# A decoder layer on one core: half of the first modulation slice's product on TensorE, and slices of 3, 5, 4 and 4 row tiles

## The chip, the cores and the metric

The kernel runs on one core of one Trainium2 chip. The metric is the device time of one launch in microseconds, as the median of several runs. Engines are named as the profile names them: PE is the matrix engine (PEld its weight loads), DVE the vector engine, ACT the scalar engine, POOL the general-purpose one, SP the engine whose queue issues most transfers.

## The reference, cut to what matters

One layer on 256 tokens of 2048 columns, all in float32. `mod` comes from one conditioning vector `c`; its first two of six parts shift and scale the first norm, whose result `h` meets the wide input matrix.

```python
mod = jax.nn.silu(c) @ w_ada[layer] + b_ada[layer]
sh1, sc1, g1, sh2, sc2, g2 = [m[:, None, :] for m in jnp.split(mod, N_MOD, axis=-1)]
h = rms_norm(x, norm1_gain[layer]) * (1.0 + sc1) + sh1
x = x + g1 * hybrid_mixer(h, positions, w_in[layer], ...)
...
proj = h @ w_in
```

`w_ada` is 2048 x 12288. The mixer (gated linear attention, sparse attention, a gated merge), the second norm, the feed-forward part and the last norm follow; the change leaves them alone.

## The kernel before

**Products.** Weights are streamed once, in chunks of at most four row tiles (128 rows) by 512 columns. Each float32 chunk is split: ACT casts it to a float32r part `hi` (L303), DVE subtracts to get the exact rest `lo` (L305), in halves of at most 1024 columns. For every row tile and each of two token tiles PE makes three products (L345 to L347): `h_hi*hi`, `h_hi*lo`, `h_lo*hi`, 512 columns each. Four halves of `hi` and of `lo` exist, and chunks are split two ahead of their products.

**The first stage.** The first 6144 columns of `w_in` are multiplied in slices over the 16 row tiles of `h` (`INIT_KTS`, 4 + 4 + 4 + 4 before), so that products can begin when a quarter of the modulation is known. A slice is 12 groups of 512 columns. The first slice leaves its results in SBUF by ACT; the later ones are added by DVE (L529). After the four slices comes the `Lr` chunk (L327, L328), and then the rest of the layer.

**The modulation of a slice.** `w_ada` is read as `(p j)`: partition p holds 16 rows j, and `sc[:, j]` is the silu of `c` for them. A piece (`Ada`) is some j of the shift and scale columns of the slice. DVE multiplies by `sc` (L283 for j = 0) and adds up (L285, a scalar_tensor_tensor) in `acc`, one instruction for each j. What remains is a sum over the partitions: `column_sums` transposes each 128 x 128 block on PE (L481) and DVE reduces it (L482); `mod_columns` then makes A and B (L455 to L457), and `modulated` makes the two parts of `h` (ACT L464, DVE L468 and L471 in the first slice).

**Order.** Nothing is scheduled behind the program's back: each engine executes in the order in which the code issues. The first slice's eight pieces come first, each issued as two transfers; the pieces of slice s + 1 are spread over the first eight groups of slice s (`ADA_DONE`, some groups earlier by `ADA_LEAD`), and DVE's work on them stands between the halves of `lo`. All raw chunks and pieces pass through six buffers in this stage, in the order of use; SP's queue loads one when its last reader is done. `first_norm` (ACT squares, POOL, ACT scales `xs`) and `transpose_x` (32 PE transposes, L491, and eight ACT copies, L495) stand ahead of the first pieces in the code, so PE does them as soon as ACT has scaled `xs`.

Of the kernel before, what the change touches and what calls it, by code (L numbers as in the profile page):

```python
# [23 lines left out]
RAW_BUFS = 3          # raw chunks of weights in flight  # L24
EARLY_RAWS = 3        # and more of them while the working tiles of later stages are not there yet
HL_BUFS = 4           # halves of split chunks
AHEAD = 2             # chunks split ahead of their products
INIT_KTS = (4, 4, 4, 4)    # row tiles of the slices of the first products
ADA_DONE = 8          # the group of a slice before which the next slice's modulation is loaded and then applied
ADA_LEAD = (0, 2, 4)  # groups by which each slice's pieces of it start early  # L30
MID = 2               # row tile of the last chunk before which the first token tile's norm goes on
# The second norm's steps (512 columns, token tile) after the first two, with p for a half of a split,
# and the steps done before each row tile of the chunks that read them.
NORM_STEPS = "p 01 11 p p 20 21 30 31"
NORM_DONE = "0000 1233 3333 4557 7777 7777"
SLOT = 3.6            # vector engine time for the threads beside a chunk, in us
# [9 lines left out]
class Mm:  # L46
    """A chunk of a weight matrix: nk row tiles of 128, nc columns, for a group of products.

    With defer, the second token tile waits until a later chunk with by_token has done the first one.
    With home, its parts are in the tiles that home makes and not in the ring of all chunks.  # L50
    """
# [19 lines left out]
class Ada:  # L71
    """A piece of w_ada: nj of every partition's 16 rows, nc columns from c0 on of nseg segments."""

    def __init__(self, c0, nc, nseg, j0, nj, acc, pre=None):
        self.c0, self.nc, self.nseg, self.j0, self.nj, self.acc, self.pre = c0, nc, nseg, j0, nj, acc, pre
        self.by_seg = False

# [6 lines left out]
class Thread:  # L84
# [6 lines left out]
    def step(self):  # L91
        """The next step's cost, which it yields, or None at the end."""
        while True:
            if self.cur is None:
                if not self.q:
                    return None
                self.cur = self.q.popleft()
            try:
                return next(self.cur) or 0.0
            except StopIteration:  # L100
                self.cur = None
# [7 lines left out]
def tile_layer(tc, x, c, positions, norm1_gain, norm2_gain, w_ada, b_ada, w_in, gate_up, gate_bias,  # L109
# [3 lines left out]
    with (  # L113
# [42 lines left out]
        # ------------------------------------------------------------ constants and small inputs  # L156
# [36 lines left out]
        # rotary tables  # L193
# [22 lines left out]
        def rstd_of(ss, n, k):  # L216
            """(ss / n + eps) ^ -0.5 in place, k columns."""
            pool.tensor_scalar(ss, ss, 1.0 / n, EPS, ALU.mult, ALU.add)
            pool.tensor_tensor(ss, ss, half[:, 0:k], ALU.pow)

        def mean_of_three(ss):
            """ss[:, :, 0] becomes the part of mean + eps of the first three of four sums, for last_rstd."""
            pool.tensor_tensor(ss[:, :, 0], ss[:, :, 0], ss[:, :, 1], ALU.add)
            pool.tensor_tensor(ss[:, :, 0], ss[:, :, 0], ss[:, :, 2], ALU.add)
            pool.tensor_scalar(ss[:, :, 0], ss[:, :, 0], 1.0 / D, EPS, ALU.mult, ALU.add)
# [5 lines left out]
        # ------------------------------------------------------------ the stream of weights  # L231
# [42 lines left out]
        def pre_ada(it):  # L274
            if it.pre:
                it.pre()
            a = it.acc()
            segs = [slice(i, i + 1) for i in range(it.nseg)] if it.by_seg else [slice(0, it.nseg)]
            for g in segs:
                for j in range(it.nj):  # L280
                    s = sc[:, it.j0 + j:it.j0 + j + 1]
                    if it.j0 + j == 0:
                        dve.tensor_scalar_mul(a[:, g], it.raw[:, j, g], s)  # L283
                    else:
                        dve.scalar_tensor_tensor(a[:, g], it.raw[:, j, g], s, a[:, g], ALU.mult, ALU.add)  # L285
                    yield

        def pre_mm(it, rests_last=False):
            """The float32 chunk into its float32r part and the exact rest, a step for each half."""
            it.hl = []  # L290
            nk, ncol = (KT, 128) if isinstance(it, Lr) else (it.nk, it.nc)
            per = min(nk, 1024 // ncol)
            home = [h().rearrange("p (k n) -> p k n", k=nk) for h in getattr(it, "home", ())]
            rests = []
            for k in range(0, nk, per):
                src = it.raw[:, k:k + min(per, nk - k)]
                m = src.shape[1]
                if home:
                    hv, lv = (h[:, k:k + m] for h in home)
                else:  # L300
                    hv, lv = (stp.tile([128, 1024], F32R, tag=v, bufs=HL_BUFS, name=name(v))[:, 0:m * ncol]
                              .rearrange("p (k n) -> p k n", k=m) for v in ("hi", "lo"))
                act.copy(hv, src)  # L303
                it.hl.append((hv, lv))
                rests.append(lambda lv=lv, src=src, hv=hv: dve.tensor_sub(lv, src, hv.bitcast(F32)))  # L305
                if not rests_last:
                    rests.pop()()
                    yield
            for rest in rests:
                yield  # L310
                rest()

        def pre(its):
            """The pieces of its, a step of each in turn: steps of one piece of w_ada depend on each other."""
# [47 lines left out]
        def run():  # L362
# [36 lines left out]
            def pre_steps(**order):  # L399
                """The next chunk's pieces, a step at a time."""  # L400
# [38 lines left out]
        # ------------------------------------------------------------ first norm and its modulation  # L439
# [13 lines left out]
        def mod_columns(ps, n, A, B, bsc, bsh, gain):  # L453
            """A = (1 + scale) * gain and B = shift of n row tiles, from ps = [shift | scale]."""
# [4 lines left out]
        def modulated(kts, h, A, B, temp, on_act, between=None):  # L459
            """The transposed tokens in xs into the parts of h at the row tiles kts."""  # L460
# [14 lines left out]
        def column_sums(blocks, dst):  # L475
            """The sums of blocks [128, 128] over the partitions, a column of dst for each."""
# [7 lines left out]
        def transpose_x():  # L484
            """xs in place into its transposes, tiles [128, 256] for the row tiles; no block is overwritten before it is read."""
            pts = {}
            for k in range(0, KT, 2):
# [5 lines left out]
                for w in sorted(pts):  # L493
                    if min(2 * w + 4, KT) <= k + 2:
                        act.copy(xs[w // 8][:, (w % 8) * S:(w % 8 + 2) * S], pts.pop(w))  # L495

        def init_columns(s, k0, nk):
            a2 = init_acc(s, nk)
            pc = cp.tile([128, 2 * nk], F32, name=name("pc"))
            column_sums([a2[:, seg, a * 128:(a + 1) * 128] for seg in range(2) for a in range(nk)], pc)  # L500
# [48 lines left out]
        def first_transposes():  # L549
            first_norm()  # L550
            transpose_x()

        items.append(Call(first_transposes))
        items.extend(init_ada(*slices[0]))
        items[-1].by_seg = True
# [32 lines left out]
        # ------------------------------------------------------------ gated linear attention  # L588
# [179 lines left out]
        # ------------------------------------------------------------ indexer  # L768
        def rope(v, nh, dh, rot, step):
            """Rotates the first rot of dh in each of nh heads, in place, on both token tiles."""  # L770
# [100 lines left out]
        # ------------------------------------------------------------ sparse attention  # L871
# [3 lines left out]
        def seg_start(i):  # L875
            """Before the first piece of a segment: what the last one left is reduced."""
# [20 lines left out]
        def reduce_rows(dst, n):  # L897
            """A slice of 512 of the sums over the partitions added to dst, on every partition."""
# [112 lines left out]
        # ------------------------------------------------------------ branches, gates and merge  # L1011
# [32 lines left out]
        def split_transposes(src, kt0, dst):  # L1044
            """Transposes [128, 2, 512] into row tiles kt0.. of the parts in dst, in two steps."""
# [94 lines left out]
        # ------------------------------------------------------------ second norm  # L1140
        def second_norm(last):
# [17 lines left out]
            def modulate(n, t, ps, a0, na):  # L1159
                """Row tiles of one token tile; the second token tile's products are on the other engine."""  # L1160
# [61 lines left out]
        # ------------------------------------------------------------ feed-forward  # L1222
# [55 lines left out]
        def final_token(t):  # L1278
            """The last norm of a token tile; the columns before the last 512 have their gain already."""
# [54 lines left out]
def constants():  # L1334
    """Constants of the shapes alone: the identity, the masks of the decay's levels, the rotary frequencies."""
# [37 lines left out]
```

## Time and profile before

| | us |
|---|---|
| median of 3 runs | 1889.79 (1889.21 to 1892.36) |
| profiled execution, first to last instruction | 1885.6 |
| median less that span | 4.2 |
| PE busy in the span | 1834.9 (97%) |
| DVE busy | 1286.0 (68%) |
| ACT busy | 854.0 (45%) |

The profiled execution has no time of its own beside its span; 4.2 us is what lies around the span if it ran as the median does. Busy shares are over the whole span, while the change touches its first sixth.

### The profile page before, as it was taken

How to read it: one execution, taken by the hardware profiler on the slowest of the kernel's cores; microseconds unless marked ns; L12 is line 12 of the kernel's file. 1: busy time of each engine (PE TensorE's matmuls, PEld its weight loads, DVE VectorE, ACT ScalarE, POOL GpSimd, SP SyncE). 2: the span in 40 equal slices, each digit the busy share in tenths (PEclk: the TensorE clock that was granted, in tenths of full speed). 3: DMA queues.
4: the chain of work that ended last, by engine and by line, in shares of the span. 5: the costliest groups of instructions: out<-in, count | busy, mean ns of one | idle time of the engine just before them, and what ended most of it. 6: DMA issues, size and time to landing. Idle time of an engine off the chain costs nothing.

```text
span 1885.6 us, 23215 instructions
## 1 busy us (share of the span) xinstructions
PE 1834.9 (97%) x9148; PEld 1510.9 (80%) x9148; DVE 1286.0 (68%) x1442; ACT 854.0 (45%) x1115; POOL 138.3 (7%) x201
## 2 busy tenths in 40 slices
PE   3999999999999999999999999999999999999998
PEld 3888888777788888888888787888788888888886
DVE  6899865788866678777777656677555444554455
ACT  4554444655645444344344446444333444334443
POOL 0000000543220110200000000000000000000002
PEclk8999999999999999999999999999999999999999
DMA  9998843543444787878888754888555555555553
GB/s 369 387 345 315 282 161 104 182 154 135 150 164 156 270 298 280 300 269 300 305 312 312 275 193 164 318 328 314 178 200 191 189 189 191 186 194 194 185 180 133
DMA packets 198046, 440.84 MB, mean 234 GB/s; under 512 B 7816, under 2 KB 14112, under 8 KB 188848
## 3 DMA queue, kind: packets, MB, share of 16 engines
q1 hardware_dynamic: 196544, 433.69, 65.5%
q10 hardware_dynamic: 1392, 5.66, 0.8%
q8 instruction: 72, 1.18, 0.2%
q14 instruction: 38, 0.31, 0.0%
HBM read 437.22 MB, written 2.10 MB: 233 GB/s over the span
## 4 chain that ended last, share of the span: by engine, by line
PE 78%; issue 12%; DVE 3%; POOL 3%; ACT 2%; DMA 1%; SPq 0%; POOLq 0%; ACTq 0%; DVEq 0%
PE pm L345 25%; PE pm L347 25%; PE pm L346 25%; DVE acc L285 1%; PE pa L1050 1%; DVE lo L305 1%; ACT hi L303 1%; POOL tm L782 1%; POOL rp L783 1%; POOL rp L780 0%; POOL rp L781 0%; PE ph L679 0%; POOL rp L779 0%; DMA raw<-in_w_ada_dram 0%; PE pa L901 0%
## 5 line engine op out<-in xcount | busy, mean ns | idle before, releaser
L305 DVE TENSOR_TENSOR lo<-raw,hi 128x1024 fp32r<-128x1024 f32 (+1 forms) x632 | 768.0, 1225 | 537.1 <-ACT hi L303 536.7
L303 ACT CAST hi<-raw 128x1024 fp32r<-128x1024 f32 (+1 forms) x632 | 652.6, 1041 | 898.8 <-PE pm L347 714.6
L345 PE MATMUL pm<-hi,h 128*128 128x512 f32 (+1 forms) x1784 | 699.0, 392 | 2.2 <-ACT h L464 1.9
L347 PE MATMUL pm<-hi,h 128*128 128x512 f32 (+1 forms) x1784 | 690.5, 387 | 0.0
L346 PE MATMUL pm<-lo,h 128*128 128x512 f32 (+1 forms) x1784 | 689.6, 387 | 0.2 <-DVE lo L305 0.2
L345 PEld LDWEIGHTS pm<-hi,h 128*128 128x128 f32 x1784 | 335.9, 188 | 70.1 <-ACT h L464 2.3
L347 PEld LDWEIGHTS pm<-hi,h 128*128 128x128 f32 x1784 | 335.5, 188 | 68.9 <-DVE h L471 0.2
L346 PEld LDWEIGHTS pm<-lo,h 128*128 128x128 f32 x1784 | 336.0, 188 | 66.1 <-DVE lo L305 0.9
L345 PE MATMUL pm<-hi,gA 128*128 128x512 f32 x608 | 242.1, 398 | 0.0
L347 PE MATMUL pm<-hi,gB 128*128 128x512 f32 x608 | 237.0, 390 | 0.0
L346 PE MATMUL pm<-lo,gA 128*128 128x512 f32 x608 | 236.8, 389 | 0.1
L285 DVE SCALAR_TENSOR_TENSOR acc<-raw,sc,acc 128x2048 f32<-128x2048 f32 (+2 forms) x122 | 218.2, 1789 | 3.5 <-DMA raw<-in_w_ada_dram 2.6
L346 PEld LDWEIGHTS pm<-lo,gA 128*128 128x128 f32 x608 | 114.2, 188 | 25.1 <-issue 1.7
L345 PEld LDWEIGHTS pm<-hi,gA 128*128 128x128 f32 x608 | 114.2, 188 | 24.7 <-issue 1.9
L347 PEld LDWEIGHTS pm<-hi,gB 128*128 128x128 f32 x608 | 114.1, 188 | 24.2
L1274 POOL TENSOR_TENSOR gC<-gC,gr 128x512 f32<-128x512 f32 x3 | 4.9, 1640 | 716.9 <-ACT pm L1272 716.9
L663 POOL TENSOR_TENSOR acc<-gC 128x512 f32<-128x512 f32 x32 | 40.0, 1260 | 34.0 <-DVE acc L672 33.6
L672 DVE TENSOR_TENSOR acc<-gB,acc 128x256 f32<-128x256 f32 x64 | 32.3, 565 | 6.9 <-ACT acc L667 6.8
L779 POOL TENSOR_TENSOR rp<-tm,cos 128x64 f32<-128x64 f32 x18 | 12.2, 677 | 297.8 <-ACT tm L927 180.1
L981 ACT ACTIVATE S<-S,mx 128x128 f32<-128x128 f32 (+1 forms) x32 | 14.3, 448 | 32.8 <-DVE mx L979 32.8
L667 ACT ACTIVATE acc<-acc 128x256 f32<-128x256 f32 x64 | 22.3, 416 | 9.7 <-POOL acc L663 9.6
L345 PE MATMUL pm<-hi,gr 128*128 128x512 f32 x64 | 24.9, 389 | 0.0
(271 smaller groups left out, 1066.6 us busy)
## 6 DMA issues: line engine op xcount, KB each, us to landing
raw<-in_w_in_dram SPq DMA_DIRECT2D x129, 1024.0 KB, 4.9
raw<-in_w_ffn_gate_up_dram SPq DMA_DIRECT2D x88, 1024.0 KB, 4.9
raw<-in_w_ada_dram SPq DMA_DIRECT2D x64, 1024.0 KB, 4.8
raw<-in_w_ffn_down_dram SPq DMA_DIRECT2D x44, 1024.0 KB, 5.2
raw<-in_w_ada_dram SPq DMA_DIRECT2D x64, 512.0 KB, 8.5
raw<-in_w_branch_gla_dram SPq DMA_DIRECT2D x16, 1024.0 KB, 5.3
raw<-in_w_branch_dsa_dram SPq DMA_DIRECT2D x16, 1024.0 KB, 5.3
raw<-in_w_merge_out_dram SPq DMA_DIRECT2D x16, 1024.0 KB, 5.4
```

Source lines behind the costliest of these rows:

```text
L285: dve.scalar_tensor_tensor(a[:, g], it.raw[:, j, g], s, a[:, g], ALU.mult, ALU.add)
L303: act.copy(hv, src)
L305: rests.append(lambda lv=lv, src=src, hv=hv: dve.tensor_sub(lv, src, hv.bitcast(F32)))
L345: pe.matmul(o, a, hv, start=it.first and k == 0, stop=False)
L346: pe.matmul(o, a, lv, start=False, stop=False)
L347: pe.matmul(o, b, hv, start=False, stop=it.last and k == it.nk - 1)
L663: pool.tensor_tensor(d, v, v[:, :, s - 1:s].to_broadcast([128, n, 2 * s]), ALU.subtract)
L667: act.activation(d, d, AF.Exp, scale=(1.0 if u else -1.0) / 16)
L672: dve.tensor_tensor(w, src, d, ALU.mult)
L782: pool.tensor_tensor(a, u[0], u[1], ALU.subtract)
L783: pool.tensor_tensor(u[0], b, co, ALU.mult)
L1050: pe.transpose(ps[:, a * S + t * 128:a * S + t * 128 + 128], src[:, t, (i * 2 + a) * 128:(i * 2 + a + 1) * 128], ident)
```

## The change

`INIT_KTS` becomes `(3, 5, 4, 4)`. For the first slice, the rows j = 1 of each of the eight pieces (two j each, 768 columns now) go to PE instead of DVE: for each of the six blocks of 128 columns a float32 product with the 128 x 128 block of raw weights as the stationary operand and `sc[:, j]`, one column, as the moving one, added up in one PSUM tile `pc`. DVE adds up the rows j = 0 alone. Then six products with a column of ones add DVE's sums over the partitions to `pc`, in place of transposes and reductions, and `mod_columns` reads PSUM. The x transposes are issued in eight steps, two behind each of the second to the fifth piece. The last piece is no longer taken segment by segment.

The second slice has five row tiles: its modulation comes in 16 pieces of one j and 1280 columns, and its groups in chunks of four and of one row tile.

```diff
-INIT_KTS = (4, 4, 4, 4)    # row tiles of the slices of the first products
+INIT_KTS = (3,5,4,4)
...
                     s = sc[:, it.j0 + j:it.j0 + j + 1]
+                    if j in it.on_pe:
+                        for i in range(2):
+                            for k in range(it.nc // 128):
+                                c = i * it.nc // 128 + k
+                                pe.matmul(state["pc"][:, c:c + 1], it.raw[:, j, i, k * 128:(k + 1) * 128], s,
+                                          start=c == 0 and it.j0 + j == it.on_pe[0], stop=False)
+                        continue
...
         def init_columns(s, k0, nk):
             a2 = init_acc(s, nk)
-            pc = cp.tile([128, 2 * nk], F32, name=name("pc"))
-            column_sums([a2[:, seg, a * 128:(a + 1) * 128] for seg in range(2) for a in range(nk)], pc)
+            blocks = [a2[:, seg, a * 128:(a + 1) * 128] for seg in range(2) for a in range(nk)]
+            if s == 0:
+                pc = state["pc"]
+                for i, b in enumerate(blocks):
+                    pe.matmul(pc[:, i:i + 1], b, ones[:, 0:1], start=False, stop=i == 2 * nk - 1)
+            else:
+                pc = cp.tile([128, 2 * nk], F32, name=name("pc"))
+                column_sums(blocks, pc)
...
-        items.append(Call(first_transposes))
-        items.extend(init_ada(*slices[0]))
-        items[-1].by_seg = True
+        items.append(Call(first_steps))
+        for i, it in enumerate(init_ada(*slices[0])):
+            it.on_pe = (1,)
+            items.append(it)
+            if 1 <= i <= 4:
+                items.append(Call(lambda: [next(state["x_steps"]) for _ in range(2)]))
         items.append(Call(first_slice))
```

PE at the start of the program, before: the last x transposes (L491), the transposes of DVE's sums (L481), and the first products.

```order
L491 MATMUL pm_198<-cc,gB_76 128x128
L491 MATMUL pm_198<-cc,gB_77 128x128
L491 MATMUL pm_198<-cc,gB_76 128x128
L491 MATMUL pm_198<-cc,gB_77 128x128
L481 MATMUL pa_254<-cc,acc 128x128 x4
L481 MATMUL pa_260<-cc,acc 128x128 x4
L345 MATMUL pm_319<-hi_247,h_105 128x512
L346 MATMUL pm_319<-lo_248,h_105 128x512
L347 MATMUL pm_319<-hi_247,h_105 128x512
```

PE in the change, the same place (the lines are numbered anew: L287 is a product with `sc`, L500 an x transpose, L513 a product with ones, L353 the first product): from the last x transposes to the first products.

```order
L500 MATMUL pm_248<-cc,gB_76 128x128
L500 MATMUL pm_248<-cc,gB_77 128x128
L500 MATMUL pm_248<-cc,gB_76 128x128
L500 MATMUL pm_248<-cc,gB_77 128x128
L287 MATMUL ph_136<-sc,raw_133 128x1 x6
L287 MATMUL ph_136<-sc,raw_168 128x1 x6
L287 MATMUL ph_136<-sc,raw_178 128x1 x6
L513 MATMUL ph_136<-ones,acc 128x1 x6
L353 MATMUL pm_354<-hi_287,h_105 128x512
L354 MATMUL pm_354<-lo_288,h_105 128x512
L355 MATMUL pm_354<-hi_287,h_105 128x512
```

Behind the last x transpose PE now has 24 small float32 products to issue before the first main product, where before it had eight transposes. At the front of its queue it has twelve, ahead of the first x transpose:

```order
L287 MATMUL ph_136<-sc,raw_118 128x1 x6
L287 MATMUL ph_136<-sc,raw_121 128x1 x6
L500 MATMUL pa_181<-cc,gB_76 128x128
L500 MATMUL pa_181<-cc,gB_77 128x128
L500 MATMUL pa_181<-cc,gB_76 128x128
L500 MATMUL pa_181<-cc,gB_77 128x128
```

The products on the first two pieces stand in front; those on pieces three to five stand between the x transposes, six behind every eight.

DVE, before, behind the first slice's `h`: the work on slice 1's pieces and the splits of groups 1 and 2 of slice 0 (L283 and L285 on pieces, L305 makes `lo`).

```order
L283 TENSOR_SCALAR acc<-raw_224,sc 128x1024
L305 TENSOR_TENSOR lo_291<-raw_229,hi_290 128x1024
L285 SCALAR_TENSOR_TENSOR acc<-raw_224,sc,acc 128x1024
L305 TENSOR_TENSOR lo_296<-raw_229,hi_295 128x1024
L285 SCALAR_TENSOR_TENSOR acc<-raw_233,sc,acc 128x1024
L305 TENSOR_TENSOR lo_306<-raw_238,hi_305 128x1024
L285 SCALAR_TENSOR_TENSOR acc<-raw_233,sc,acc 128x1024
L305 TENSOR_TENSOR lo_311<-raw_238,hi_310 128x1024
```

DVE in the change, the same place (L291, L293 on pieces, L313 makes `lo`):

```order
L291 TENSOR_SCALAR acc<-raw_219,sc 128x1280
L293 SCALAR_TENSOR_TENSOR acc<-raw_240,sc,acc 128x1280
L313 TENSOR_TENSOR lo_321<-raw_265,hi_320 128x1024
L313 TENSOR_TENSOR lo_325<-raw_265,hi_324 128x512
L293 SCALAR_TENSOR_TENSOR acc<-raw_274,sc,acc 128x1280
L293 SCALAR_TENSOR_TENSOR acc<-raw_284,sc,acc 128x1280
L313 TENSOR_TENSOR lo_339<-raw_315,hi_338 128x1024
L313 TENSOR_TENSOR lo_343<-raw_315,hi_342 128x512
L293 SCALAR_TENSOR_TENSOR acc<-raw_328,sc,acc 128x1280
L293 SCALAR_TENSOR_TENSOR acc<-raw_331,sc,acc 128x1280
```

Two pieces of 1280 columns, one instruction each, now stand ahead of a group's two `lo` halves (1024 and 512 columns), where one piece of two instructions of 1024 columns stood beside two halves of 1024.

## Rows read from the trace of the kernel before

**Rows 1.** The page: its head, and busy time, share and instructions by engine.

```profile
span 1885.6 us, 23215 instructions
PE 1834.9 (97%) x9148; PEld 1510.9 (80%) x9148; DVE 1286.0 (68%) x1442; ACT 854.0 (45%) x1115; POOL 138.3 (7%) x201
```

**Rows 2.** Timeline of PE (start, length): first of slice 1; end of the stage.

```profile
106.94 0.39 PE L345 MATMUL pm<-hi,h 128*128 128x512 f32 x1
...
305.31 0.39 PE L347 MATMUL pm<-hi,h 128*128 128x512 f32 x1
305.54 0.39 PE L327 MATMUL pm<-h,hi 128*128 128x512 f32 x1
```

**Rows 3.** Timeline of all engines, the first 45 us; bracketed: idle before, and releaser.

```profile
12.16 0.75 DVE L283 TENSOR_SCALAR acc<-raw,sc 128x1024 f32<-128x1024 f32 x1 [4.16 <-DMA raw<-in_w_ada_dram]
...
15.27 19.16 DVE L285 SCALAR_TENSOR_TENSOR acc<-raw,sc,acc 128x1024 f32<-128x1024 f32 x16 [1.03 <-DMA raw<-in_w_ada_dram]
...
19.05 0.90 PE L491 MATMUL pa<-cc,gB 128*128 128x128 f32 x3 [1.42 <-ACT gB L451]
...
19.75 1.06 PE L491 MATMUL pm<-cc,gB 128*128 128x128 f32 x4
...
23.56 0.60 PE L491 MATMUL pa<-cc,gB 128*128 128x128 f32 x4
...
34.10 1.99 ACT L303 CAST hi<-raw 128x1024 fp32r<-128x1024 f32 x2 [7.04 <-DMA raw<-in_w_in_dram]
...
35.69 0.69 DVE L482 TENSOR_REDUCE pc<-pa 128x4 f32<-128x512 f32 x1 [0.67 <-PE pa L481]
...
37.52 0.80 PE L345 MATMUL pm<-hi,h 128*128 128x512 f32 x1 [1.87 <-ACT h L464]
...
39.08 0.33 PEld L345 LDWEIGHTS pm<-hi,h 128*128 128x128 f32 x1
...
42.19 0.75 DVE L283 TENSOR_SCALAR acc<-raw,sc 128x1024 f32<-128x1024 f32 x1
```

**Rows 4.** Stretches of 10 us, columns as in the first row.

```profile
core 0: us, PE busy (x) PEld busy (x) DVE busy (x) ACT busy (x) POOL busy (x), PEclk, DMA share, GB/s
0.00:10.00 10.00, 0.69 (x2) 0.36 (x2) 0.32 (x1) 4.71 (x13) 0.43 (x6) 1.00 0.82 307
10.00:20.00 10.00, 1.42 (x6) 1.13 (x7) 6.62 (x6) 5.80 (x9) 2.97 (x5) 1.00 1.04 384
20.00:30.00 10.00, 4.59 (x28) 4.35 (x26) 9.47 (x8) 4.30 (x8) 0.00 (x0) 0.99 1.05 387
30.00:40.00 10.00, 4.48 (x13) 2.99 (x14) 8.94 (x18) 4.53 (x7) 0.00 (x0) 0.50 1.05 387
40.00:50.00 10.00, 10.00 (x38) 8.10 (x37) 9.90 (x12) 4.60 (x6) 0.00 (x0) 0.82 1.05 387
```

**Rows 5.** Weight loads by line and shape: count, busy us, mean ns of one.

```profile
L345 PEld LDWEIGHTS pm<-hi,h 128*128 128x128 f32 x1784 | 335.9, 188 | 70.1 <-ACT h L464 2.3 <-issue 2.1 <-ACT hi L303 1.1
...
L693 PEld LDWEIGHTS pa<-acc 128*128 128x128 f32 x16 | 2.4, 190 | 0.3
...
L698 PEld LDWEIGHTS pa<-acc 128*64 128x64 f32 x32 | 2.2, 137 | 0.5
```

**Rows 6.** Timeline of PE around 372 us: two kinds of float32 product.

```profile
372.36 0.60 PE L693 MATMUL pa<-acc 128*128 128x128 f32 x4
372.89 0.68 PE L698 MATMUL pa<-acc 128*64 128x64 f32 x8
```

**Rows 7.** DVE by line and shape, 37 to 310 us: the split at two widths.

```profile
L305 DVE TENSOR_TENSOR lo<-raw,hi 128x876 fp32r<-128x876 f32 x1 | 1.1, 1074 | 0.2 <-ACT hi L303 0.2
...
L305 DVE TENSOR_TENSOR lo<-raw,hi 128x292 fp32r<-128x292 f32 x1 | 0.5, 464 | 1.1 <-ACT hi L303 1.1
```

**Rows 8.** Chain that ended last, 145 to 165 us: start, length, engine, tile.

```profile
155.37 1.14 DVE lo L305
156.50 1.20 DVE acc L285
```

More of the change, by code (lines that the diff above doesn't have):

```diff
@@ L76, in __init__ @@
         self.by_seg = False
+        self.on_pe = ()
 class Call:
@@ L486, in transpose_x @@
             pts = {}
+            yield
             for k in range(0, KT, 2):
@@ L495, in transpose_x @@
                         act.copy(xs[w // 8][:, (w % 8) * S:(w % 8 + 2) * S], pts.pop(w))
+                yield
         def init_columns(s, k0, nk):
             a2 = init_acc(s, nk)
-            pc = cp.tile([128, 2 * nk], F32, name=name("pc"))
-            column_sums([a2[:, seg, a * 128:(a + 1) * 128] for seg in range(2) for a in range(nk)], pc)
+            blocks = [a2[:, seg, a * 128:(a + 1) * 128] for seg in range(2) for a in range(nk)]
[6 more added lines that the diff above has]
+                column_sums(blocks, pc)
             kk = slice(k0, k0 + nk)
@@ L548, in tile_layer, with first_steps @@
             k0 += nk
-        def first_transposes():
+        def first_steps():
+            state["pc"] = psum_held()
             first_norm()
-            transpose_x()
-        items.append(Call(first_transposes))
-        items.extend(init_ada(*slices[0]))
-        items[-1].by_seg = True
+            state["x_steps"] = transpose_x()
+            next(state["x_steps"])
+        items.append(Call(first_steps))
[4 more added lines that the diff above has]
+                items.append(Call(lambda: [next(state["x_steps"]) for _ in range(2)]))
         items.append(Call(first_slice))
```

## The prediction

> **What bounds the kernel now.** I read the page first: PE is busy for 97% of a span of 1885.6 us [rows 1], so a gain must come from when PE starts, or from waits of PE. Then the timeline of the start and of the stage's end: the first product starts at 37.52 us [rows 3], slice 1 at 106.94, and the stage's last product ends where `Lr` begins, at 305.54 [rows 2]. The reader is to see that from 37.52 on PE hardly waits: the 864 products of slices 1 to 3 (36 groups of 24) take 198.6 us, 0.230 us each with all gaps. Everything behind 305.54 is work of PE that the change leaves alone, so I let the shift of that point pass through to the end one to one. The question is thus one number: when does the last product of the first stage end?
>
> Before 37.52 the chain is: pieces of `w_ada`, DVE's 16 instructions on them (15.27 to 34.4), transposes and reductions to 36.38, A and B, `h`. Beside it the first weight chunk lands only at 34.10 (ACT's cast waited 7.04 us for it) [rows 3]. The transfers run at 384 to 387 GB/s from 10 us on, whatever the engines do [rows 4]: the queue is full. That is the second limit.
>
> **The yardstick.** After the change slices 1 to 3 have 13 row tiles, 936 products: 936 x 0.230 = 215.2 us. So the stage ends as before if slice 0 ends (the end of its 216 products) at 305.5 - 215.2 = 90.3 us.
>
> **Part 1: when the first product starts.** The pieces hold 0.79 MB instead of 1.05 MB, so the first lands some 0.7 us earlier than the 12.16 of now, at 11.5 us, and one more each 2.03 us at 387 GB/s, the eighth at 25.7. DVE has one instruction for each piece and is done about 27. That would save much; but PE now has 54 products with one moving column, none of which the trace shows.
>
> Their price. A float32 product is recorded as two passes, each with its own load of the stationary block (L693: eight products in the code, 16 loads [rows 5]). One moving column costs next to nothing, so the load of 128 columns sets the pace. The mean load takes 190 ns for 128 columns and 137 for 64 [rows 5]: 0.83 ns a column, so 106 ns for 128 beside a fixed part that overlaps. Upper bound: L693, which loads 128 and streams 128 columns, steps (0.60 - 0.27)/3 = 0.11 us a pass (0.27 is the length of one, and the last of the four hardly overlaps) [rows 6]; with fewer streamed columns a pass can't be dearer. Lower bound: if the load went at the pace at which a main product streams 512 columns in 0.23 us, 0.45 ns a column, a pass would take 0.058 us. L698, with half the columns on both sides, steps (0.68 - 0.22)/7 = 0.066 [rows 6], which fits the dear end. I take 0.107 a pass, 0.21 us a product at the full clock, 0.43 at the lower level: the load of a main product is recorded with 0.33 us at 39.08 [rows 3] and 0.188 in the mean [rows 5], and four transposes take 1.06 us at 19.75 and 0.60 at 23.56 [rows 3], 0.213 and 0.11 each.
>
> The sum on PE. The first two pieces' 12 products are done at 16.7 even at the lower level (2.56 us each from 11.5). The x transposes wait for ACT until 19.05 as now [rows 3]; nothing moves there. From 19.05 PE has 32 transposes and 42 products in a row: 3.5 + 8.8 = 12.3 us at the full clock, plus some 0.9 if the clock rises only during the first of them (before, the step fell at about 23): 32.3. No data is late for it. From the end of the sums to the first product it now takes 37.52 - 36.38 = 1.1 us: **first product at 33.4**, 4.1 us earlier. What is late next is PE itself; at a lower price it would be the first weight chunk: 9.5 MB in all, landed at 28, cast by 29.6, first product at 30.
>
> By the way the clock stands: PE ran only transposes between 19 and 25 us, and the step fell to 0.11 while they ran, with the granted clock at 0.99 for 20 to 30 us, and 0.50 for 30 to 40, after a pause [rows 3, 4]; the main products before 43 us ran at the lower level. The Trainium skill (TensorE: Matmul & The Clock Gate, PE-mode transpose) says that the full clock does not engage for transposes. By that rule the 32 transposes would stay at 0.213 us, and the first product would come at 35.8 instead of 33.4; this trace disagrees, and I go by it.
>
> **Part 2: slice 0 itself.** A group is now 18 products, 4.14 us of PE. For each of the first eight groups DVE has two pieces of 1280 columns and two halves of `lo`. In the chain `lo` of 1024 columns takes 1.14 us and an addition of 1024 takes 1.20 [rows 8]; a column costs (1074 - 464)/584 = 1.04 ns [rows 7]. So: 2 x 1.47 + 1.14 + 0.61 = 4.69, plus about 0.1 because the two additions to one `acc` now stand side by side (16 in 19.16 us at the start, four of them half as long [rows 3], are slower than 1.20 each): 4.8 us. **DVE is slower than PE in these groups**, 4.8 against 4.14, where before it had 2 x (1.14 + 1.20) = 4.68 against 24 x 0.230 = 5.5. Ahead of this stands the first group's own work: 37.52 to 42.19 for four row tiles [rows 3], 3.5 for three. The `lo` of the ninth group is ready at first product + 3.5 + 8 x 4.8 = + 41.9 us; the last four groups, in which DVE has no more than PE, take 16.6. Slice 0 ends 58.5 us behind its first product, of which 8.8 are PE waiting for DVE. With 33.4: 91.9 us, 1.6 us later than the yardstick.
>
> **The floor under it.** Even if PE's small products cost nothing, the data must come: 2.46 MB of `x` and constants, 6.29 of first pieces, nine chunks of 0.79, 16 pieces of 0.66: 26.3 MB before the ninth group can start. 10.8 MB are there at 30 us [rows 4], the other 15.5 take 40 us at 387 GB/s: 70.1. From the bytes to a `lo` it is some 3.3 us (in the trace the first chunk's last byte, 11.9 MB in all, would be there at 32.9; cast at 34.10, cast 1.0, `lo` 1.14): 73.4 us, and slice 0 ends no earlier than 90.0. So the gain can't be more than 0.3 us, however cheap part 1 is. Before, the larger slice 0 hid this.
>
> **Smaller edits.** DVE's reductions and PE's transposes of slice 0's sums go; their time is in part 1. DVE gets 12 more halves of `lo` in all (9 for 8 in a group of each slice pair), inside the 4.8 above and in slice 1, where a group of 30 products gives PE 6.9 us and DVE has 1.14 x 2 + 0.61 + 1.28 of additions + about 1.8 of pieces = 6.0: hidden, at 0.9 us of margin a group. SP's loads of buffers wait for PE too, but in the sum above PE frees each some us before the queue is due.
>
> **The sum.** 91.9 + 215.2 = 307.1 against 305.5: +1.6 us on a median of 1889.8, whose profiled span is 4.2 us shorter: **1891.4 us**, no change that can be told. (About 0.2%, 3.8 us, is what a measurement here tells from no change.)
>
> **Rivals.**
> - *The clock stays at the lower level until the main products.* Then from 19.05: 32 x 0.213 + 42 x 0.43 = 24.9, first product at 45.1, slice 0 ends at 103.6: +13.3, 1903 us. For it: no row shows the clock beside a stretch of one-column products, and it took until 43 us before for the main products themselves to get the full clock. Against: from 19.05 on PE has no pause, and the transposes raised the clock. It decides from a first product at 35.6 on (+3.8). Chance 0.28.
> - *In between*: all 32 transposes stay at 0.213 and the products run at 0.21 (19.05 + 6.8 + 8.8 + 1.1 = 35.8: +4.0, 1893.8; chance 0.04, since the step of 0.11 speaks against it; the rule named in part 1 would do this), or the clock falls again in the 24 small products behind the last transposes (up to +5, first product at 36 to 39, 1894 to 1897; chance 0.08).
> - *Slice 1 starves*: the one-tile chunk's cast and `lo` (0.6 + 0.6) come too late in each of 12 groups: up to +14. Against: four halves hold the next chunk while PE has 5.5 us on the four-tile one. Chance 0.04.
> - *Faster by over 3.8 us*: slice 0 would have to end before 86.5, so transfers at some 415 GB/s from 10 us on, where five rows show 387 at most, and the cheap end of the load's price as well. Chance 0.06.
>
> **How the numbers follow.** Forecast 0.50, with its floor at 1889.5 and its dear end at 1893.5; slower 0.28 + 0.04 + 0.08 + 0.04 = 0.44; faster 0.06. The range goes from 1888.5 (the floor, less a microsecond of spread) to 1903 (the lower clock): about 0.16 lies outside.
>
> **What would show it.** In the profile after: two load records for each small product, about 0.11 us apart at the full clock; first product at 33 to 34 us; a granted clock near 1 from about 23 us on; PE waiting for DVE's `lo` in groups 1 to 8, 8 to 9 us in all; slice 0's end at 91 to 93; 0.230 a product from there. Wrong if the loads pair up faster and the first product comes at 30, if the clock row shows 0.5 until 45 us, or if DVE's pairs of additions take under 2.9 us.

## The result, and the profile after

The changed kernel takes 1902.61 us (1901.45 to 1904.95, six runs), against 1890.4 for the kernel before on the same chip (1887.59 to 1893.44, six runs): a ratio of 1.0062, interval 1.0050 to 1.0074, so 9.5 to 14 us slower. The range held this, the likeliest case did not: 1891.4 was forecast, and the first rival (the clock stays at the lower level) had been priced at 1903. That was also the range's upper end, so the range held by 0.4 us. One of four executions of the run with more work, below, took 5762.82 us and is left out.

The page of the profile after: its head, and busy time, share and instructions of each engine.

```profile
span 1901.8 us, 23510 instructions
PE 1861.1 (98%) x9250; PEld 1534.3 (81%) x9250; DVE 1276.6 (67%) x1442; ACT 856.3 (45%) x1128; POOL 135.6 (7%) x201
```

This execution took 1903.61 us, 1.8 more than its span, and the later executions of the kernel before take as much more than theirs (1.7 to 1.9 us). So most of the 4.2 us that I had put around the span of before was the difference of two executions. PE is busier than before [rows 1] and the kernel is slower: the added busy time, 26.2 us, is mostly the small products (23.6 us in all).

The timeline of the kernel after, all engines (start, length, engine, line; bracketed: idle before, and releaser).

```profile
10.46 5.53 PE L287 MATMUL ph<-sc,raw 128*128 128x1 f32 x24 [2.75 <-DMA raw<-in_w_ada_dram]
...
17.50 0.90 PE L500 MATMUL pa<-cc,gB 128*128 128x128 f32 x3 [1.19 <-ACT gB L459]
18.20 1.06 PE L500 MATMUL pm<-cc,gB 128*128 128x128 f32 x4
19.05 2.56 PE L287 MATMUL ph<-sc,raw 128*128 128x1 f32 x12
...
30.68 1.06 PE L500 MATMUL pm<-cc,gB 128*128 128x128 f32 x4
31.53 7.68 PE L287 MATMUL ph<-sc,raw 128*128 128x1 f32 x36
...
39.07 2.70 PE L513 MATMUL ph<-ones,acc 128*128 128x1 f32 x12
41.80 0.16 DVE L463 TENSOR_TENSOR mods<-ph,cols 128x3 f32<-128x3 f32 x1 [13.76 <-PE ph L513]
42.98 0.79 PE L353 MATMUL pm<-hi,h 128*128 128x512 f32 x1 [1.21 <-ACT h L472]
...
46.24 0.62 PE L353 MATMUL pm<-hi,h 128*128 128x512 f32 x1
...
46.94 0.39 PE L355 MATMUL pm<-hi,h 128*128 128x512 f32 x1
...
104.86 0.39 PE L353 MATMUL pm<-hi,h 128*128 128x512 f32 x1
...
319.64 0.39 PE L335 MATMUL pm<-h,hi 128*128 128x512 f32 x1
```

Twelve records of L287 are six products, and they take 2.56 us from 19.05 on and still 7.68/3 = 2.56 us from 31.53 on: 0.213 us a record, the price at the lower of the two levels of PE's clock (1.2 and 2.4 GHz). Four transposes take 1.06 us at 18.20 and still 1.06 at 30.68, where before they had come down to 0.60 by 23.56 [rows 3]. So from 17.50 to 41.7 PE works without a pause and never gets faster. DVE stands idle for 13.76 us before L463: in the kernel before it was the last to finish [rows 3], here PE is. The first main product starts at 42.98 instead of 37.52 [rows 3], slice 1 (104.86) 2.1 us earlier than before, and the stage ends at 319.64 instead of 305.54 [rows 2], 14.1 us later.

Stretches of 10 us of the kernel after, columns in the first row.

```profile
core 0: us, PE busy (x) PEld busy (x) DVE busy (x) ACT busy (x) POOL busy (x), PEclk, DMA share, GB/s
10.00:20.00 10.00, 8.23 (x38) 7.88 (x38) 3.68 (x4) 6.31 (x9) 1.49 (x5) 1.00 1.04 370
20.00:30.00 10.00, 10.00 (x49) 10.00 (x50) 4.08 (x4) 1.17 (x2) 0.00 (x0) 1.00 0.97 346
30.00:40.00 10.00, 10.00 (x49) 10.00 (x48) 0.00 (x0) 4.00 (x7) 0.00 (x0) 1.00 0.66 211
40.00:50.00 10.00, 8.34 (x29) 6.35 (x28) 7.91 (x15) 3.04 (x5) 0.00 (x0) 1.00 0.50 156
```

PE and its loads are busy for all of 20 to 40 us, and the transfers fall from 387 GB/s [rows 4] to 211 and 156. The waits of SP's queue from 20 to 50 us (releaser: us in total, times, longest) say why:

```profile
SPq L271 <- PE ph L287: 10.7, 4, 3.7
...
SPq L273 <- PE ph L287: 5.3, 2, 3.3
```

The six raw buffers are held by pieces and chunks that PE has not come to. The head start of the transfers is lost while PE is late.

The clock column reads 1.00 here although the records have the lower level's lengths. The column counts what lies ahead of the trace's first recorded change of level as 1.00, and in this trace the first one is a rise at 46.7 us, in the first group's main products: there their records go from 0.62 to 0.39 us. In the kernel before the first one is a rise at 23.1 us, where the step of the transposes fell, and 10 to 20 us reads 1.00 there as well [rows 4]. The prediction had named this column as its sign; it read near 1 as forecast, while the level was the rival's. So ahead of the first recorded change I read the level from the steps: 0.213 and 0.11 us for a load or a transpose, 0.43 and 0.23 for a main product.

### The profile page after: what moved, and what is told of

It is laid out like the page before. It is cut to its first block, busy times and chain, and to the rows that moved or that the text cites. A ratio compares the mean times of both kernels' runs of the same rounds, so it can differ in the third digit from the quotient of the medians.

```text
span 1901.8 us, 23510 instructions
## 1 busy us (share of the span) xinstructions
PE 1861.1 (98%) x9250; PEld 1534.3 (81%) x9250; DVE 1276.6 (67%) x1442; ACT 856.3 (45%) x1128; POOL 135.6 (7%) x201
## 4 chain that ended last, share of the span: by engine, by line
PE 81%; issue 9%; POOL 3%; DMA 2%; DVE 2%; ACT 2%; POOLq 0%; ACTq 0%; SPq 0%; DVEq 0%
PE pm L353 25%; PE pm L355 25%; PE pm L354 25%; DMA raw<-in_w_in_dram 2%; DVE lo L313 1%; PE ph L287 1%; ACT hi L311 1%; PE pa L1071 1%; POOL tm L803 1%; POOL rp L802 0%; POOL rp L804 0%; POOL rp L801 0%; DVE acc L693 0%; PE pa L922 0%; PE pa L994 0%
## 5 line engine op out<-in xcount | busy, mean ns | idle before, releaser
L313 DVE TENSOR_TENSOR lo<-raw,hi 128x1024 fp32r<-128x1024 f32 (+3 forms) x644 | 768.0, 1204 | 539.2 <-ACT hi L311 538.6
L311 ACT CAST hi<-raw 128x1024 fp32r<-128x1024 f32 (+3 forms) x644 | 654.7, 1027 | 902.7 <-PE pm L355 687.8
L353 PE MATMUL pm<-hi,h 128*128 128x512 f32 (+1 forms) x1784 | 700.2, 392 | 7.3 <-ACT gC L543 3.1
L353 PEld LDWEIGHTS pm<-hi,h 128*128 128x128 f32 x1784 | 336.1, 188 | 77.4 <-ACT gC L543 4.5
L353 PE MATMUL pm<-hi,gA 128*128 128x512 f32 x608 | 242.1, 398 | 0.0
L293 DVE SCALAR_TENSOR_TENSOR acc<-raw,sc,acc 128x2048 f32<-128x2048 f32 (+3 forms) x112 | 209.5, 1871 | 12.0 <-DMA raw<-in_w_ada_dram 11.7
L353 PEld LDWEIGHTS pm<-hi,gA 128*128 128x128 f32 x608 | 114.2, 188 | 24.6 <-issue 1.9
L353 PE MATMUL pm<-hi,gr 128*128 128x512 f32 x64 | 24.9, 389 | 0.0
```

Of the source, the lines that this page charges most:

```text
L353: pe.matmul(o, a, hv, start=it.first and k == 0, stop=False)
```

## The experiments

Three kernels first take the change apart; "the stage ends" is the start of `Lr` (305.54 before, 319.64 after).

**The slices alone** (the kernel before with one line changed).

```diff
-INIT_KTS = (4, 4, 4, 4)
+INIT_KTS = (3, 5, 4, 4)
```

> The kernel before with slices of 3, 5, 4 and 4 row tiles and nothing else: DVE does all 16 rows of the first slice, and PE's transposes and DVE's reductions sum over the partitions. Theory A (the small products of PE, at the lower clock, hold up the first product; the slices alone are about neutral): first product at 30.5 to 32 us, slice 0 ends at 90 to 93, time +0 to +3 us against before. Theory B (the small first slice itself costs, since DVE or the transfers can't feed it, and the late first product is covered): slice 0 takes as long as in the change (62 us), and the time is most of the change's +12, +8 us or more.

Measured: 1893.77 us against 1889.58, ratio 1.0019 (1.0010 to 1.0027). First product at 31.95, slice 1 at 92.86, the stage ends at 307.68, 2.1 us later than before. Slice 0 took 60.9 us, as theory B has it, with a first product as early as theory A has it. In its chain from 38 to 82 us (start, length, what) the transfers stand in front:

```profile
by line: DMA raw<-in_w_in_dram 51.6%; DMA raw<-in_w_ada_dram 12.7%; DVE lo L305 6.9%; ACT hi L303 6.3%; issue 5.5%; PE pm L345 4.8%; PE pm L346 4.3%; PE pm L347 4.2%; PE pa L481 2.5%; ACT gA L527 1.1%; SPq L270 0.7%; ACTq L303 0.3%; DVEq L2
...
54.75 7.62 DMA raw<-in_w_in_dram
...
65.41 7.62 DMA raw<-in_w_in_dram
```

**The products on PE alone** (the change with the slices of before).

```diff
-INIT_KTS = (3,5,4,4)
+INIT_KTS = (4, 4, 4, 4)
```

> The change with its slices put back to 4, 4, 4 and 4: pieces of 1 MB, eight small products each. Theory A: from the second piece on PE has 32 transposes of 0.213 and 56 small products of 0.427 us: first product at 49 to 51 us, slice 0 as long as before (66 to 69 us), time +11 to +14 us. Theory B: the first product is late too, but it costs little; time within 4 us of before.

Measured: 1901.0 us, ratio 1.0062 (1.0050 to 1.0075). First product at 49.59, slice 1 at 118.41, the stage ends at 317.0, 11.5 us later. So the products on PE alone bring a loss of the change's size, though with 64 small products on raw weights here for 48 there.

**The change without the 48 small products** on raw weights; the six with ones stay, and the first of them starts the sum.

```diff
                     if j in it.on_pe:
-                        for i in range(2):
-                            for k in range(it.nc // 128):
-                                ...
                         continue
```

> The change without the 48 products with raw weights (the rows j = 1 of the first slice are left out of the modulation, so the output is not the reference's); the six products with ones stay. It shows the floor that transfers and DVE set with these slices. Theory A: first product at 29.5 to 31 us, slice 0 ends at 89 to 92, time -1 to +2 us. Theory B: slice 0 takes 60 us or more from its first product, time +5 us or more.

Measured: 1894.01 us, ratio 1.0025 (1.0015 to 1.0035). First product at 33.68, slice 1 at 94.35, the stage ends at 309.14. The expected first product was missed by some 3 us, and the expected time with it: DVE starts on the second piece at 15.97, 4.5 us behind the first, and on the eighth at 28.61 (2.11 us a piece from there, where I had 2.03 and an eighth landed at 25.7), and the six products with ones came after a pause, at the lower level. PE's timeline of this run:

```profile
22.46 1.06 PE L495 MATMUL pa<-cc,gB 128*128 128x128 f32 x4
23.32 0.74 PE L495 MATMUL pm<-cc,gB 128*128 128x128 f32 x4
29.77 2.69 PE L508 MATMUL ph<-ones,acc 128*128 128x1 f32 x12 [5.72 <-DVE acc L288]
33.68 0.80 PE L348 MATMUL pm<-hi,h 128*128 128x512 f32 x1 [1.21 <-ACT h L467]
...
309.14 0.39 PE L330 MATMUL pm<-h,hi 128*128 128x512 f32 x1
```

Here the same 32 transposes, with nothing between them, do get faster at 23.3 us, as before. So the 14.1 us of the change are 2.1 from the slices, 1.5 from the rest of the new start, and 319.64 - 309.14 = 10.5 from the 48 small products (each from one profiled execution).

The next three ask whether it is the clock, and what raises it.

**Wide products.** The operands are swapped: `sc` is stationary, the raw weights move, 384 columns at a time; two products a piece instead of six, and their rows are turned into columns at the end.

```diff
-                            for k in range(it.nc // 128):
-                                c = i * it.nc // 128 + k
-                                pe.matmul(state["pc"][:, c:c + 1], it.raw[:, j, i, k * 128:(k + 1) * 128], s, ...)
+                            pe.matmul(state["pc"][32 * i:32 * i + 1, 0:it.nc], s, it.raw[:, j, i, :], ...)
```

> The change with the two operands swapped: the column of silu(c) is stationary and the raw weights move, 384 columns to a product, two products to a piece in place of six; the sums stand in rows and are turned to columns by six products of one partition. The streaming time at one clock is about that of the loads it replaces (2 x 2 passes x 0.32 us at the full clock). Theory A, if a stream of moving columns brings the clock up: two passes of 0.32 us, first product at 33 to 36 us, time +1 to +4 us. If the clock stays at the lower level here too: first product at 42 to 45, time +9 to +13. Theory B: +9 us or more either way.

Measured: 1889.76 us, ratio 1.0005 (0.9996 to 1.0014): no change from the kernel before that can be told. PE's timeline:

```profile
18.66 1.44 PE L285 MATMUL ph<-raw,sc 128*1 128x384 f32 x4
...
21.63 0.81 PE L285 MATMUL ph<-raw,sc 128*1 128x384 f32 x4
22.38 0.66 PE L498 MATMUL pa<-cc,gB 128*128 128x128 f32 x4
...
32.77 0.79 PE L351 MATMUL pm<-hi,h 128*128 128x512 f32 x1 [1.14 <-ACT h L470]
...
308.42 0.39 PE L333 MATMUL pm<-h,hi 128*128 128x512 f32 x1
```

A piece costs 1.44 us and then 0.81, the step falling at 21.3. First product at 32.77, slice 1 at 93.65. The stage ends at 308.42, 11.2 us earlier than in the change and still 2.9 later than before, about the slices' own loss. Two things have changed at once here: the level rises, and a piece is cheaper at either level. Its two products write to different partitions of PSUM and run side by side (in the trace those of the piece at 21.63 start 8 ns apart). So this run alone does not single out the level; the next one does.

**More work at the start of the changed kernel.** Behind the six small products of each piece PE makes one more, of a constant 128 x 496 operand, into unused columns.

```diff
+                        pe.matmul(state["pc"][:, 16:512], ident, cc[:, 0:496], start=False, stop=False)
                         continue
```

> The change with one more product for each of the eight pieces, behind its six small ones: the identity against 496 columns of the constants, added to columns of the PSUM tile that nothing reads. Theory A, with the clock as the cause of the price: if these wide products bring the clock up, a pass of a small product takes 0.107 us, transposes step 0.11, a wide product costs 0.83: first product at 35.5 to 38 us, time 4 to 8 us under the change although PE has more to do. If the loads cost 0.213 a pass at either clock, or the clock stays down: first product at 48 us or later, time 5 us or more over the change.

Measured: 1898.81 us, ratio 1.0047 (1.0032 to 1.0062). PE's timeline:

```profile
14.88 2.56 PE L287 MATMUL ph<-sc,raw 128*128 128x1 f32 x12
17.30 2.00 PE L289 MATMUL ph<-cc 128*128 128x496 f32 x2
...
20.80 1.73 PE L287 MATMUL ph<-sc,raw 128*128 128x1 f32 x12
22.39 1.08 PE L289 MATMUL ph<-cc 128*128 128x496 f32 x2
23.30 0.60 PE L501 MATMUL pa<-cc,gB 128*128 128x128 f32 x4
...
24.18 1.40 PE L287 MATMUL ph<-sc,raw 128*128 128x1 f32 x12
...
39.40 0.79 PE L354 MATMUL pm<-hi,h 128*128 128x512 f32 x1 [1.21 <-ACT h L473]
```

With eight more products the first main product comes 3.6 us earlier than in the change, and the stage ends at 315.12, 4.5 earlier. The same six small products take 2.56 us before the clock rises and 1.40 (a step of 0.11) after. That is the test of the cause: nothing was taken away, and for the small products only the level differs. The gain is smaller than expected (a first product at 35.5 to 38 us, 4 to 8 us of time): the level rises only at 21.5 us, in the third piece, and the added products cost 1.8 us each ahead of that and 0.9 after, 9.1 in all.

**The kernel before with ten filler products** of 512 columns in PE's idle time, eight behind the x transposes and two ahead of the first main products.

```diff
+        items.append(Call(lambda: filler(8)))
         items.append(Call(first_slice))
...
             init_columns(*slices[0])
+            filler(2)
```

> The kernel before with ten wide products (identity against 512 columns of the constants, into a PSUM tile that nothing reads) in PE's idle time: eight behind the x transposes, two behind the transposes of the sums. Theory A (the lower clock costs the kernel before some 3 us at its first products): the main products step 0.227 from the start, the sums' transposes 0.11, first product at 36.5 to 37.5, slice 1 at 102.5 to 104, time -3 to -4 us. If the clock falls again before the first product, or the start is paced by DVE and ACT and not by PE: 0 to -1 us.

Measured: 1887.92 us, ratio 0.9986 (0.9977 to 0.9995): about 2.6 us faster than the kernel before. PE's timeline:

```profile
25.07 7.03 PE L553 MATMUL pm<-cc 128*128 128x512 f32 x16
32.55 0.63 PE L481 MATMUL pa<-cc,acc 128*128 128x128 f32 x4 [0.44 <-DVE acc L285]
...
34.46 1.88 PE L553 MATMUL pm<-cc 128*128 128x512 f32 x4
36.49 0.51 PE L345 MATMUL pm<-hi,h 128*128 128x512 f32 x1 [0.15 <-ACT h L464]
```

The main products step by 0.23 us from 38 us on, where before they ran at the lower level until 43. Slice 1 starts at 103.84 instead of 106.94 [rows 2], and the stage ends 3.1 us earlier.

The last ones ask what paces slice 0, where I had named DVE. All have the slices (3, 5, 4, 4) on the kernel before.

**DVE's additions of every second piece of slice 1 left out**, the transfers kept.

```diff
+                    if it.nc == 640 and (it.j0 + j) % 2:
+                        yield
+                        continue
```

> Slices of 3, 5, 4 and 4 with DVE's additions for every second piece of slice 1 left out (its modulation is not the reference's); the transfers stay. Theory T (transfers pace slice 0): its groups still start 5.2 to 5.4 us apart, slice 1 at 91.5 to 93.5, time within 1.5 us of the slices alone. Theory D (DVE paces it, as the prediction has it): groups 4.1 to 4.4 us apart, slice 1 at 84 to 87, time 5 us or more under the slices alone.

**Every second piece of slice 1 left out altogether.**

```diff
-            return [Ada(...) for j0 in range(0, 16, nj)]
+            return [Ada(...) for j0 in range(0, 16, nj * (1 + (s == 1)))]
```

> Slices of 3, 5, 4 and 4 with every second piece of slice 1 left out altogether, transfer and addition (its modulation is not the reference's). Theory T: 1.44 MB for a group take 3.7 us, under PE's 4.1: groups 4.1 to 4.3 us apart, slice 1 at 83 to 87, time 5 to 8 us under the slices alone, and the half without additions alone gives none of it. Theory D: the same times here, but reached by the half without additions too.

Measured: 1894.44 us, ratio 1.0021 (1.0012 to 1.0030), without the additions; 1885.6, ratio 0.9974 (0.9965 to 0.9983), without the pieces. A stretch of 10 us: the slices alone, then without the additions, then without the pieces.

```profile
60.00:70.00 10.00, 8.12 (x35) 6.05 (x34) 9.02 (x8) 4.75 (x8) 0.00 (x0) 1.00 1.04 393
```

```profile
60.00:70.00 10.00, 8.12 (x35) 6.04 (x34) 5.88 (x6) 5.08 (x8) 0.00 (x0) 1.00 1.04 392
```

```profile
60.00:70.00 10.00, 10.00 (x46) 8.29 (x45) 6.58 (x7) 6.80 (x11) 0.00 (x0) 1.00 1.03 382
```

DVE falls from 9.0 to 5.9 of 10 us, and PE is busy for 8.12 as in the slices alone; a group still starts every 5.3 us on average, and slice 1 at 92.50 instead of 92.86. With half the pieces PE is busy for 10.00 of 10, a group takes 4.08, slice 1 starts at 85.32 and the stage ends at 300.13. A group moves one chunk and two pieces, 2.10 MB, which at 392 GB/s is 5.35 us. The transfers pace slice 0, and not DVE. Nor does a wait for free buffers show: the DMA engines are busy throughout (a share of 1.04, next to the last number of the row), and 392 GB/s is close to the highest rate of any stretch of these runs, 395.

**The pieces of a slice over ten groups, or nine, instead of eight.**

```diff
-ADA_DONE = 8
+ADA_DONE = 10
```

> The kernel before with the slices (3, 5, 4, 4), and the pieces of each next slice spread over ten groups of a slice instead of eight; nothing is left out and no byte is added. Theory (transfers pace slice 0): a group of the first ten carries 1.6 pieces instead of two, 1.83 MB instead of 2.10, so groups start 4.7 us apart instead of 5.33 at 390 GB/s, slice 0 takes about 10 x 4.7 + 2 x 4.14 + the first group's 3.5 less the overlap, some 56 to 58 us instead of 60.9, slice 1 starts at 88 to 90 us, and the time is 3 to 5 us below that of the slices alone. Rival (the six buffers' loop or another wait of fixed length sets the 5.3 us): groups stay 5.2 to 5.4 us apart and slice 1 starts later than 92. Rival (DVE): a group with two pieces still takes 4.8 us and one with a single piece 3.3, 4.2 us in the mean, bounded by PE: slice 1 before 87.

> The kernel before with the slices (3, 5, 4, 4), and the pieces of each next slice spread over nine groups of a slice instead of eight; nothing is left out, no byte is added, and slice 2's pieces still begin after slice 1's sums (with ten groups they began before them and overwrote them). Theory (transfers pace slice 0): a group of the first nine carries 1.78 pieces instead of two, 1.95 MB instead of 2.10, so groups start 5.0 us apart in the mean instead of 5.33 at 390 GB/s; the wait before the ninth group goes, slice 0 ends 1.5 to 2 us earlier than the 92.9 of the slices alone, 90.5 to 91.5, and the time is 1 to 2 us lower, 1891 to 1893. Rival (another wait of fixed length sets the 5.3 us): groups stay 5.2 to 5.4 us apart and there are nine such groups, slice 1 at 94. Rival (DVE paces): no change of more than 0.3 us in slice 0, since its additions stay the same in sum.

Measured: 1902.33 us with ten, 1899.03 with nine. Both miss what was expected, because the code issues the work on pieces two groups ahead of the products: in both runs slice 2's first piece goes to the same part of `acc` before PE has taken slice 1's sums, so slice 1's modulation is spoilt, and PE waits for DVE (7.0 us ahead of L481 with ten). Only the groups ahead of that can be read: with ten, eight groups from 43.70 to 80.04 take 4.54 us each instead of 5.3, those with fewer pieces 4.2 to 4.4. Fewer bytes a group shorten it, but so do fewer additions, so these runs do not tell transfers from DVE; the run without the additions does. The same two settings with wide products (1899.76 and 1896.31 us) have the same defect. Whether spreading the pieces pays stays open.

## Why the prediction was right and wrong

**The step of the forecast that failed is in part 1: the level of the clock.** "3.5 + 8.8 = 12.3 us at the full clock" was the sum for 32 transposes and 42 small products. Both prices were right (0.107 a pass taken, 0.11 measured in the run with more work; 0.213 at the lower level), but the level was not: the stretch ran at 0.213 throughout. I had argued from a row in which PE ran transposes alone and got faster [rows 3], and from PE's having no pause. The run without small products shows that the row was read rightly for transposes alone; what it did not carry was the step to a mixture. The first rival said just this, with a first product at 45.1; it came at 42.98, mostly because the second half of the transposes' input was ready at 17.50 and not at 19.05 [rows 3]. That its time, 1903, is the time measured is partly luck: the first product came 2.1 us earlier than in that rival, and slice 0 took 61.9 us where it had 58.5. The chance of 0.28 was low for it: all that spoke against it was a row of another operation.

The rule that I set against this trace is the one on transposes (Trainium skill, TensorE: Matmul & The Clock Gate, PE-mode transpose): by it the full clock does not engage for them. In the changed kernel they do stay at 0.213; in the kernel before, without small products, and with filler they reach 0.11. So it does not hold here as a rule of transposes.

**Part 2: the length was nearly right and the cause wrong.** I had 3.5 + 8 x 4.8 + 16.6 = 58.5 us for slice 0, with DVE as the slower engine. It took 61.9, and 60.7 to 61.0 in four other runs with these slices and their pieces, whether the first product came at 31.95 or at 39.40. With the slices alone the first group took 7.1 where the sum had 3.5 (its products ran mostly at the lower level), the second 4.1, seven groups 5.34 each instead of 4.8, and three 4.1. DVE's 4.8 was read rightly (9.0 busy of 10 us is 4.8 of 5.34); what it left out is that the bytes of a group take longer. The prediction had these bytes in its floor, two pieces of 0.66 MB and a chunk of 0.79, 5.4 us at 387 GB/s, but summed them only over the whole slice. The six buffers let the transfers run only a little ahead of PE (SP's queue waits 16.0 us for L287 in the kernel after), so a late first product does not buy a shorter slice. The chain of waits of the kernel after (start, length, what) shows transfers too, where I had expected `lo`:

```profile
55.28 6.89 DMA raw<-in_w_in_dram
...
65.21 9.20 DMA raw<-in_w_in_dram
...
77.44 7.59 DMA raw<-in_w_in_dram
```

In the table of waits, 46 to 105 us (engine, line, releaser: us in total, times, longest), PE's own waits name ACT's evacuations:

```profile
ACT hi L311 <- DMA raw<-in_w_in_dram: 24.5, 7, 5.1
...
PE pm L353 <- ACT gC L543: 3.1, 2, 2.4
PE pm L353 <- ACT gA L543: 2.8, 3, 1.0
```

That is the same cause one step on: ACT's cast waits for its chunk, and the evacuation that PE needs stands behind the cast in ACT's queue, as the chain shows ahead of the product at 87.23:

```profile
86.09 0.61 ACT hi L311
86.70 0.49 ACT gA L543
```

**The floor was right in kind and too early in size.** I had slice 0 end at 90.0 at best by the transfers. The slices alone end it at 92.86. Its transfers ran at 375, 382, 373 and 376 GB/s from 10 to 50 us, and at 290 before, instead of 307 and then 384 to 387 [rows 4]: 17.96 MB by 50 us, and the other 8.34 MB of the 26.3 at 392 GB/s until 71.3 instead of 70.1. The ninth group started at 75.23 instead of 73.4; and it still waited, so that the last four groups took 17.6 us instead of 16.6. So with the level risen the change would by estimate have been near the slices' own loss, +2 to +4 us, not +1.6; the run with wide products, where it rose, ends the stage 2.9 us later than before.

**What held.** Slices 1 to 3 took 319.64 - 104.86 = 214.8 us, 215.2 forecast; slice 1 did not starve on its one-tile chunks. The shift of the stage's end passed through to the time, but only to some 2 us: it lies inside the interval for the slices alone (2.1 against 1.9 to 5.1) and the filler (3.1 earlier against 0.9 to 4.3), just outside for the change (14.1 against 9.5 to 14.0) and for wide products (2.9 against -0.8 to 2.6). What follows the stage took 1579.4 to 1587.0 us in the profiled executions, 1580.1 in that of the kernel before, so a single span is not to be set against a median.

## What to carry to other kernels

A price per instruction is not enough on PE: ask at which level of the clock the stretch will run, and take as evidence only a row with the same mixture of operations. Products with one moving column can be turned round, so that the narrow operand is stationary and the wide one moves: 1.44 or 0.81 us a piece here at the lower and the full level, instead of 2.56 or 1.40, and the level rose. When one engine is relieved at a place that transfers feed, work out the bytes of a group over the rate of the trace first: here it gave the pace (5.35 us) that the sum over DVE's instructions missed.

## What the runs showed of the hardware

- PE was busy without a pause from 17.50 to 41.7 us with one-column float32 products and transposes, and stayed at the lower level (1.2 GHz); in the kernel before it rose while PE ran transposes alone (at 23.1), with wide products while PE ran products of 384 moving columns (at 14.4; it fell at 17.9, after a pause of PE, and rose again at 21.3), with more work once products of 496 columns stood among the small ones (at 21.5), and in the kernel after in the main products (at 46.7). Why it does not rise in the small products stays open.
- The clock column reads 1.00 ahead of a trace's first recorded change of level (46.7 us in the kernel after), so the column alone would have misled; the steps of the records show the level.
- Two products with one stationary column that write to different PSUM partitions ran side by side: 8 ns apart in the run with wide products.
- Transfers ran some 1 to 7% slower while the first slice's pieces had three row tiles: 359 to 379 GB/s from 10 to 20 us in all such runs against 384 to 392 with four, and 380 to 382 from 20 to 30 us, where they did not wait for PE, against 387. No run separates the row length from the count of transfers.
